# Keys and values of an encoder block: two plain products of x, or one product formed from seven quarter products

## The chip, the core and the metric

The kernel runs on one core of one Trainium2 chip. The metric is the device time in microseconds of one execution, taken as the median of several runs. The core has five engines with queues of their own: PE multiplies matrices (into PSUM), DVE (VectorE), ACT (ScalarE) and POOL (GpSimd) work on vectors of 128 partitions, and SP issues most of the transfers. An engine takes its instructions in the order of its queue, and one that waits holds up all behind it.

## What is computed

One layer of a bidirectional encoder on 1024 rows of 1024 columns, all in float32. What matters here is the combined projection of the normalised rows, and what its columns are for:

```python
h = rms(x, norm1_g)
p = h @ w_in                        # columns: qk of mLSTM, v, o, 16 gates, attention q, k, v
mix_a = mlstm_group(silu(dwconv(p_qk)), p_v, p_o, p_gates, ...)
mix_b = diff_attention_group(p_q, p_k, p_va, ...)    # q and k are normalised per head of 64
x = x + concat(mix_a, mix_b) @ w_out
x = x + square(relu(rms(x, norm2_g) @ w_ff1)) @ w_ff2
```

Of these columns, "values" below are the 512 of `p_v` (mLSTM), "keys" the 512 of the attention's k, "queries" the 512 of its q, and "gates" the 16 input and forget gates.

## The kernel before, in words

Every float32 product is made of three products of a shorter type: each operand is split into a high part (a copy by ACT that rounds to `F32R`) and a low part (operand minus high part, a subtraction by DVE or POOL), and PE adds high x high, high x low and low x high in PSUM. The factor `1/rms` of a row is not put on x but applied to the outputs (`rcol`, by rows; `rb`, the same copied to all partitions, by columns); the weight of the norm is put on x in the split.

The start of the kernel, which the change rewrites, goes in four parts.

Values. Eight PSUM banks `pv` hold the eight blocks of 128 rows. For each of the eight blocks k of 128 columns of x, SP loads `xT[k]`, ACT makes `hhi[k]` (line 221) and DVE `hlo[k]` (222), weights are loaded by pairs of k and split (171, 173, 174; the first pair by halves, with DVE's cast at 212), and PE adds 24 matmuls of 512 columns (239). Then the rows of x are loaded again in row order by POOL's queue (251), ACT sums their squares (252), DVE and POOL turn the sums to `rcol` (253, 89), POOL's queue stores them to DRAM and loads them again copied to all partitions, as `rb` (259, 260). The values are scaled by `rcol` as they leave PSUM and are stored to `vm_dram` (265 to 268).

Keys with gates. `key_weights` (404 to 406) loads and splits four tiles of 2 x 528 columns. For each block of rows PE makes two accumulations of 256 and 272 columns (`mm3`, lines 138 to 140); DVE takes the gates out (436), `head_norm` (339 to 349) copies the keys to SBUF, sums squares per head and scales. `head_turn` (368 to 381) transposes the normalised keys and stores them.

Queries. `row_block` does the same with four tiles of 2 x 512 columns. Between their matmuls, `step()` lets the pending generators go on, one piece at a time: the turns of keys, then `gates()`, which transposes the gates, scans them and stores the rows that the mLSTM heads load later.

After this, `proj` and `columns` form the convolution's inputs, one tile of 128 columns at a time. In that part the order on the engines is written out by hand: `when(t, f)` puts a piece of work at a time of the code's clock, which goes on by one every 12 matmuls, and the pieces are issued in the order of these times.

In the first three parts the order of the work is that of the program text, as far as the framework's own ordering keeps it. The tiles take their room from pools by tags; a tile that takes the room of another waits until all reads and writes of that one are done.

## Time and profile before

| what | value |
|---|---|
| median of 3 runs | 1238.62 us (1238.03 to 1239.58) |
| the profiled execution's own time | 1239.08 us |
| its span, first to last instruction | 1236.9 us |
| granted TensorE clock, mean over the span | 1.000 |
| ACT busy | 621.7 us (50%) |
| SP's queue (q1) | 154.11 MB, 38.8% of the transfer engines' time |
| POOL's queue (q0) | 25.70 MB |
| DMA in all | 212.77 MB, 172 GB/s |

A row of the timeline reads: start in us, duration in us, engine, line of the code, operation, output tile <- input tiles, shapes, how many instructions the row merges, and in brackets how long the engine had been idle and for whom. A row of the groups reads: line, engine, operation, tiles and shapes, count, then busy time in us and the mean of one in ns, then the idle time before them and who ended it. A row of the waits reads: engine, tile and line, the one waited for, then us in total, how often, and the longest. The durations of PE's matmuls overlap (a row of 0.39 us follows the last by 0.23), so a matmul's cost is taken from start to start.

### The profile page before, as it was taken

The numbers are of one execution on the slowest core, as the hardware profiler recorded it, in microseconds if no ns is written. First come the engines' busy times: TensorE is split into PE (matmuls) and PEld (weight loads), VectorE is DVE, ScalarE is ACT, GpSimd is POOL, SyncE is SP. The second block draws the span as 40 slices with busy tenths as digits, with TensorE's granted clock in tenths as the row PEclk, the third lists the DMA queues.
The fourth block names the chain that finished last, engine by engine and source line by source line (L and its number), as shares of the span: only waits on it lengthen the run. The fifth ranks groups of instructions, "written<-read, shape, count | busy, mean of one in ns | idle before, by whom it ended". The sixth has DMA issues, their size and how long they took to land.

```text
span 1236.9 us, 17075 instructions
## 1 busy us (share of the span) xinstructions
PE 1228.3 (99%) x6397; PEld 1029.4 (83%) x6397; DVE 817.0 (66%) x1154; ACT 621.7 (50%) x1070; POOL 240.7 (19%) x268
## 2 busy tenths in 40 slices
PE   9999999999999999999999999999999999999998
PEld 8998788888878878888887888888888888888887
DVE  6335668895267796774789886766655765468654
ACT  7334437777356676664465454454544433333332
POOL 1133513473334363321000000000000000014001
PEclk9999999999999999999999999999999999999999
DMA  9514262364364585526545773534459655445732
GB/s 346 207 41 165 45 226 81 113 157 123 124 223 160 167 287 162 177 92 234 184 145 166 244 247 136 170 130 157 148 212 343 245 165 193 147 132 163 221 111 94
DMA packets 102750, 212.77 MB, mean 172 GB/s; under 512 B 9096, under 2 KB 21896, under 8 KB 102664
## 3 DMA queue, kind: packets, MB, share of 16 engines
q1 hardware_dynamic: 78164, 154.11, 38.8%
q10 hardware_dynamic: 15272, 31.89, 6.7%
q0 software_dynamic: 9232, 25.70, 6.3%
q8 instruction: 50, 0.82, 0.3%
q14 instruction: 32, 0.26, 0.1%
HBM read 153.36 MB, written 58.30 MB: 171 GB/s over the span
## 4 chain that ended last, share of the span: by engine, by line
PE 90%; DVE 4%; DMA 2%; ACT 1%; issue 1%; POOL 1%; ACTq 0%; SPq 0%; DVEq 0%; POOLq 0%
PE z L1746 8%; PE z L1745 8%; PE z L1744 8%; PE m L1415 7%; PE m L1417 7%; PE m L1416 7%; PE pav L1018 4%; PE pva L889 4%; PE pv L239 4%; PE pl L978 4%; PE pw L138 3%; PE pw L140 2%; PE pw L139 2%; PE pj_c L138 2%; PE pj_c L140 2%; PE pj_c L139 2%
## 5 line engine op out<-in xcount | busy, mean ns | idle before, releaser
L1789 POOL TENSOR_TENSOR zx<-zx,res 128x512 f32<-128x512 f32 x4 | 8.7, 2181 | 492.0 <-DVE zx L1787 492.0
L1746 PE MATMUL z<-wbh,wa0l 128*128 128x512 f32 x224 | 87.4, 390 | 0.1
L983 DVE CUSTOM_DVE_ANT_0 l<-pl,toe 128x1024 f32<-128x1024 f32 x64 | 76.3, 1221 | 16.6 <-PE pl L978 15.9
L1744 PE MATMUL z<-wbh,wa0h 128*128 128x512 f32 x224 | 87.2, 389 | 0.0
L1745 PE MATMUL z<-wbl,wa0h 128*128 128x512 f32 x224 | 87.1, 389 | 0.0
L1745 PE MATMUL z<-wel,wa1h 128*128 128x512 f32 x224 | 87.1, 389 | 0.0
L1744 PE MATMUL z<-weh,wa1h 128*128 128x512 f32 x224 | 87.1, 389 | 0.0
L1746 PE MATMUL z<-weh,wa1l 128*128 128x512 f32 x224 | 87.1, 389 | 0.0
L1328 ACT ACTIVATE wbh<-g 128x1024 fp32r<-128x1024 f32 x28 | 29.7, 1061 | 90.2 <-PE z L1746 53.0
L1328 ACT ACTIVATE weh<-g 128x1024 fp32r<-128x1024 f32 x28 | 29.7, 1061 | 90.2 <-PE z L1746 53.4
L989 ACT ACTIVATE l<-l,sm 128x1024 f32<-128x1024 f32 x64 | 73.2, 1149 | 0.5 <-DVE sm L983 0.5
L1331 DVE TENSOR_TENSOR wel<-g,weh 128x1024 fp32r<-128x1024 f32 x28 | 35.2, 1257 | 56.6 <-ACT weh L1328 56.6
L1464 ACT ACTIVATE sq<-sq 128x512 f32<-128x512 f32 x48 | 30.2, 630 | 82.5 <-DVE sq L1503 65.7
L1331 DVE TENSOR_TENSOR wbl<-g,wbh 128x1024 fp32r<-128x1024 f32 x28 | 35.4, 1265 | 53.5 <-ACT wbh L1328 53.3
L1018 PEld LDWEIGHTS pav<-v,at 128*128 128x128 f32 x512 | 61.5, 191 | 3.4 <-issue 1.1
L1018 PE MATMUL pav<-v,at 128*128 128x128 f32 x512 | 62.7, 275 | 0.0
L978 PE MATMUL pl<-kk,q 64*128 64x512 f32 x384 | 55.3, 410 | 0.9 <-DVE sm L983 0.9
L138 PE MATMUL pj_c<-hhi,w_c 128*128 128x512 f32 x128 | 53.1, 414 | 0.0
L138 PE MATMUL pw<-mix,hi_wo 128*128 128x512 f32 x128 | 52.0, 406 | 0.0
L140 PE MATMUL pj_c<-hhi,w_c 128*128 128x512 f32 x128 | 50.3, 393 | 0.0
L139 PE MATMUL pj_c<-hlo,w_c 128*128 128x512 f32 x128 | 50.1, 391 | 0.0
L140 PE MATMUL pw<-mix,lo_wo 128*128 128x512 f32 x128 | 50.0, 391 | 0.0
(450 smaller groups left out, 3575.1 us busy)
## 6 DMA issues: line engine op xcount, KB each, us to landing
g<-g_dram SPq DMA_DIRECT2D x56, 512.0 KB, 3.9
g_dram<-gs SPq DMA_DIRECT2D x64, 256.0 KB, 4.4
g_dram<-sq ACTq DMA_DIRECT2D x42, 256.0 KB, 2.2
kk<-k_dram POOLq DMA_DIRECT2D x16, 512.0 KB, 6.0
raw_wo<-in_w_o_dram SPq DMA_DIRECT2D x16, 512.0 KB, 4.9
re<-in_w_dram SPq DMA_DIRECT2D x16, 512.0 KB, 4.4
ro<-in_w_dram SPq DMA_DIRECT2D x16, 512.0 KB, 3.8
zt<-in_w_dram SPq DMA_DIRECT2D x16, 512.0 KB, 3.9
```

Source lines behind the costliest of these rows:

```text
L138: nc.tensor.matmul(out, ahi, bhi, start=start, stop=False)
L139: nc.tensor.matmul(out, ahi, blo, start=False, stop=False)
L140: latest[0] = nc.tensor.matmul(out, alo, bhi, start=False, stop=stop).ins
L978: nc.tensor.matmul(it.pl[x][:, sl], hd.q[r, i, qi * P : (qi + 1) * P], hd.kk[r, j, sl], start=n == 0, stop=n == 2)
L983: nc.vector.tensor_tensor_reduce(lt, it.pl[m], hd.toe[:, off : off + S], 1.0, 3.0e38, ALU.add, ALU.min, it.sm[:, m : m + 1])
L1018: nc.tensor.matmul(it.pav[:, 0:P], at, it.head.v[:, c], start=c == 0, stop=c == NC - 1)
L1415: nc.tensor.matmul(p, wh, xh, start=go, stop=False, skip_group_check=True)
L1416: nc.tensor.matmul(p, wh, xl, start=False, stop=False, skip_group_check=True)
L1417: nc.tensor.matmul(p, wl, xh, start=False, stop=stop and k == 3, skip_group_check=True)
L1744: nc.tensor.matmul(p, wh, gh, start=go, stop=False, skip_group_check=True)
L1745: nc.tensor.matmul(p, wh, gl, start=False, stop=False, skip_group_check=True)
L1746: nc.tensor.matmul(p, wl, gh, start=False, stop=end, skip_group_check=True)
```

## The change

Keys and values are computed together. With x cut into quarters (rows 0 to 511 and 512 to 1023; columns 0 to 511 and 512 to 1023: A11, A12, A21, A22) and the weights of keys and of values each cut into an upper and a lower half (k0, k1; v0, v1), the four output quarters are formed from seven products of quarters instead of eight. Eight of the fourteen operands are sums: of x, A21+A22, A11-(A21+A22), A11-A21 and A12+A11-(A21+A22), each times the norm's weight; of the weights, v0-k0, v0-k0-v1, v1-v0 and v0-k0-v1+k1 (`t1` to `t4`). Each sum is split into high and low part like any operand.

The seven products go into eight PSUM banks, four `X` and four `Z`. Keys of the upper rows are products one and two; the others come from running sums that ACT copies out of `X` and DVE adds to `Z`. Product six adds into the banks of `Z` that hold product three, after these have been read (`keep3` and the sum behind it). Each product is 16 groups of three matmuls of 512 columns.

The order of this part is written out by hand on all engines: `at(t, f)` collects pieces of work, and they are issued in the order of their times t, which are planned microseconds. `pe(p, i)` is the planned time of group i of product p (both from 0). A core of the diff; it is cut at the marks.

```diff
+    order.enter_context(tc.manual_schedule())
...
+        G = 0.682
+        T0 = 5.0
+
+        def pe(p, i):
+            return T0 + G * (16 * p + i)
...
+        def hi(dst, x, g=None):
+            if g is None:
+                nc.scalar.activation(dst[0], x, AF.Copy)
+            else:
+                nc.scalar.activation(dst[0], x, AF.Copy, scale=g)
+
+        def lo(dst, x, eng=nc.vector):
+            eng.tensor_tensor(dst[1], x, dst[0].bitcast(F32), op=sub)
+
+        def lo_g(dst, x, g):
+            nc.vector.scalar_tensor_tensor(dst[1], x, g, dst[0].bitcast(F32), op0=mult, op1=sub)
...
+        def vt(out, a, b, op, eng=nc.vector):
+            eng.tensor_tensor(out, a, b, op=op)
+
+        def mul_add(out, x, g, y, op=add):
+            nc.vector.scalar_tensor_tensor(out, x, g, y, op0=mult, op1=op)
...
+        for j in range(4):
+            t = 18.5 + 2.6 * j
+            at(t, hi, (hs[j],), x22[j], g1[4 + j])
+            at(t + 0.5, vt, kr[j], v0[j], kr[j], sub, nc.gpsimd)
+            at(t + 0.6, hi, A22[j], x22[j], g1[4 + j])
+            at(t + 0.8, mul_add, hs[j], x21[j], g1[j], hs[j])
+            at(t + 1.6, hi, SB[j], hs[j])
+            at(t + 1.7, lo_g, A22[j], x22[j], g1[4 + j])
+            at(t + 1.9, whi, "t1", j, kr[j])
+            at(t + 2.3, lo, SB[j], hs[j])
+            at(t + 2.6, wlo, "t1", j, kr[j], nc.gpsimd)
...
+        for j in range(4):
+            at(29.0 + 1.4 * j, mul_add, hs[j], x11[j], g1[j], hs[j], sub)
+            at(29.8 + 1.4 * j, hi, A21[j], hs[j])
+            at(30.5 + 1.4 * j, lo, A21[j], hs[j])
...
+        for j in range(4):
+            at(31.0 + 1.3 * j, lambda j=j: vt(kr[j], kr[j], v1[j], sub, nc.gpsimd))
+            at(32.6 + 1.5 * j, whi, "t2", j, kr[j])
+            at(33.5 + 1.5 * j, wlo, "t2", j, kr[j])
...
+        for j in range(4):
+            at(36.0 + 1.3 * j, vt, d[j], x11[j], x21[j], sub, nc.gpsimd)
+            at(41.0 + 1.3 * j, lambda j=j: vt(v0[j], v1[j], v0[j], sub, nc.gpsimd))
+            at(38.5 + 1.4 * j, hi, SB[j], d[j], g1[j])
+            at(39.2 + 1.4 * j, lo_g, SB[j], d[j], g1[j])
+            at(42.2 + 1.4 * j, whi, "t3", j, v0[j])
+            at(46.5 + 1.3 * j, wlo, "t3", j, v0[j], nc.gpsimd)
+            at(44.5 + 0.8 * j, mul_add, x12[j], x12[j], g1[4 + j], hs[j])
...
+            at(50.5 + 0.1 * j, load_k1, j)
+            at((40.5, 49.0)[j // 2] + 0.8 * (j % 2), lambda j=j: whi("v1", j, v1[j]))
+            at(51.7 + 1.3 * j, lambda j=j: wlo("v1", j, v1[j], nc.gpsimd))
+            at(50.5 + 1.0 * j, hi, A21[j], x12[j])
+            at(51.2 + 1.0 * j, lo, A21[j], x12[j])
+            at(57.0 + 1.3 * j, lambda j=j: vt(kr[j], kr[j], k1b[j], add, nc.gpsimd))
+            at(59.5 + 1.3 * j, whi, "t4", j, kr[j])
+            at(62.2 + 1.3 * j, wlo, "t4", j, kr[j], nc.gpsimd)
...
+        plan = (
+            (X, A11, "k0", True, False), (Z, A12, "k1", True, True), (Z, SB, "t1", True, False),
+            (X, A21, "t2", False, False), (X, SB, "t3", False, False), (Z, A21, "v1", False, True),
+            (X, A22, "t4", False, True),
+        )
...
+        for t in range(4):
+            e = lambda p, t=t: pe(p, 9.9 + 2 * t) + 0.3
+            at(e(0), lambda t=t: nc.scalar.activation(zs[0][:, t], X[t], AF.Copy))
+            at(e(1), lambda t=t: nc.vector.tensor_tensor(zs[0][:, t], Z[t], zs[0][:, t], op=add))
+            at(e(3), keep, t)
+            at(e(4), keep3, t)
+            at(e(4) + 0.7, lambda t=t: nc.vector.tensor_tensor(vr[4 + t], Z[t], vr[4 + t], op=add))
+            at(e(5), values, t)
...
+        for t in range(NC):
+            at(41.3 + 2.6 * t, row_load, t)
+            at(44.0 + 2.6 * t, row_square, t)
+        at(63.0, row_factor)
+        at(65.5, row_turn)
...
+        for i, (slot, t1, t2) in enumerate(((0, 67.3, 70.2), (1, 67.4, 71.6), (2, 72.9, 74.6), (4, 76.0, 77.4))):
+            at(t1, query_room, i, slot)
+            at(t2, lambda i=i: hi(wqg[i], wqg[i][2]))
+            at(t2 + 1.2, lambda i=i: lo(wqg[i], wqg[i][2]))
```

`row_turn` is the store of the row factors and the load of `rb`, still on POOL's queue; row slices of x are now loaded by SP's queue (`row_load`). Half of the keys' weights and a quarter of x are loaded a second time (`load_k1`, `load_x21`). The query weights' raw tiles take the room of `kr`, the raw weights of keys in which the sums of weights are formed.

Behind this part the loop that formed keys with gates forms queries with gates, in the same shapes and with the same `step()`; `row_block` is gone. The keys, which already lie in SBUF, are normalised by `key_norm`, the squares with the row factor as scale. The first piece of `gates()` runs ahead of `proj`, and its other pieces are put into the hand-written table of the part after it:

```diff
+    for n in range(9):
+        heapq.heappush(table, (0.3 + 1.2 * n, 10**6 + n, next, (gate_steps, None)))
```

More of the change, by code (lines that the diff above doesn't have):

```diff
@@ new lines, in key_norm, with end @@
+    def key_norm(t):
+        zt = zs[t // 4][:, t % 4]
+        sq = kgp.tile([P, 8, 64], F32, tag="zsq", name=f"zsqk{t}", bufs=2)
+        nc.scalar.activation(sq.rearrange("p a b -> p (a b)"), zt, AF.Square, scale=rcol[:, t : t + 1])
+        ss = kgp.tile([P, 8], F32, tag="zss", name=f"zssk{t}", bufs=2)
+        nc.vector.tensor_reduce(ss, sq, axis=mybir.AxisListType.X, op=ALU.add)
+        last = nc.vector.tensor_scalar(ss, ss, 64 * EPS, None, op0=ALU.add)
+        rsqrt(ss, ss, 8)
+        with tc.issue_after(last.ins):
+            norm_end()
+        z8 = zt.rearrange("p (a b) -> p a b", b=64)
+        def end():
+            nc.vector.tensor_scalar(ss, ss, rcol[:, t : t + 1], None, op0=ALU.mult)
+            nc.vector.tensor_tensor(z8, z8, ss[:, :, None].to_broadcast([P, 8, 64]), op=ALU.mult)
+        ends.append(end)
@@ L575, in hybrid_block_kernel @@
+        if t == 4:
+            pending.append(head_turn(kgp2, "zz", 4, zs[1], 1, False))
+            pending.append(head_turn(kgp2, "zz", 4, zs[2], 0, True))
+    norm_end()
+    gate_steps = gates()
+    next(gate_steps)
     pj0 = proj(w_c[4], "c4")
```

360 lines of the change are left out of this document (218 added, 142 removed).

## Prediction

> **What bounds the kernel now.** I read the page's busy shares first, then the waits of PE, then PE's timeline around the changed stage.
>
> ```profile
> span 1236.9 us, 17075 instructions
> PE 1228.3 (99%) x6397; PEld 1029.4 (83%) x6397; DVE 817.0 (66%) x1154; ACT 621.7 (50%) x1070; POOL 240.7 (19%) x268
> ```
>
> ```profile
> PE pv L199 <- POOL ones L76: 1.1, 1, 1.1
> ```
>
> PE is busy 99% of the span, and the longest wait that any PE instruction has is 1.1 us, at the very start. So the end is set by the number of matrix columns that PE streams: a matmul taken away anywhere is worth its whole pitch, and any microsecond in which PE is made to wait is lost in full. Both halves of that sentence decide this change.
>
> The chain of waits and PE's timeline give the stage's parts:
>
> ```profile
> 5.17 43.84 PE pv L239 x192
> ```
>
> ```profile
> 48.84 0.28 PE L138 MATMUL pkg<-w_kg,hhi 128*128 128x256 f32 x1
> ...
> 96.90 0.29 PE L140 MATMUL pkg<-w_kg,hlo 128*128 128x272 f32 x1
> 97.49 0.39 PE L140 MATMUL pqa<-w_qa,hlo 128*128 128x512 f32 x1
> 98.17 0.39 PE L140 MATMUL pqa<-w_qa,hlo 128*128 128x512 f32 x1
> ```
>
> The values are 192 matmuls of 512 columns from 5.17 to 48.84: 43.67/192 = 0.2274 us each, 0.68 per group of three (97.49 to 98.17 is the same step among the queries). Keys with gates run from 48.84 to 97.2 in 384 matmuls of 256 and 272 columns, with 16 transposes between. The queries after them are again 192 matmuls of 512.
>
> How full the helpers are is in the windows of the stage (columns: window, length, then busy time of PE, PEld, DVE, ACT, POOL, granted clock, DMA share, GB/s):
>
> ```profile
> 0.00:10.00 10.00, 8.71 (x39) 7.70 (x40) 4.63 (x8) 5.70 (x8) 1.11 (x11) 1.00 0.79 276
> 10.00:20.00 10.00, 10.00 (x46) 8.29 (x45) 8.88 (x15) 7.71 (x9) 1.29 (x2) 1.00 1.03 411
> ...
> 60.00:70.00 10.00, 10.00 (x85) 10.00 (x85) 3.41 (x8) 2.64 (x4) 2.86 (x2) 1.00 0.01 2
> ```
>
> While values run, DVE is busy 8.88 of 10 us; while keys run, only 3.41. The present stage has its vector work early and little later on; POOL does 1.3 to 2.9 us in ten.
>
> **PE's work.** Keys and values are each 8 x 8 x 512 columns times three: 384 matmuls, 384 x 0.2274 = 87.3 us. Seven quarter products of 16 (block, row) pairs times three are 336, or 76.4 us. Gates with queries have the shapes and the count that gates with keys had, so they cancel, and so do the transposes of keys and queries. PE's saving is 48 x 0.2274 = 10.9 us. With PE alone, keys and values that start at 5.17 end at 92.5 before and at 81.6 after.
>
> **The first product.** It starts later.
>
> ```profile
> 3.44 0.43 DVE L212 CAST w_v<-raw_v 128x512 fp32r<-128x512 f32 x1 [2.61 <-DMA raw_v<-in_w_v_dram]
> 4.39 0.72 ACT L221 ACTIVATE hhi<-xt,vecs 128x512 fp32r<-128x512 f32 x1 [1.72 <-DMA xt<-in_xT_dram]
> 6.62 0.63 ACT L230 ACTIVATE w_v<-raw_v 128x512 fp32r<-128x512 f32 x1
> 8.01 1.43 DVE L222 SCALAR_TENSOR_TENSOR hlo<-xt,vecs,hhi 128x512 fp32r<-128x512 f32 x2
> ```
>
> Now DVE casts the first weights (3.44) while ACT is still waiting for x, and the first matmul goes 5.17, when ACT's 0.72 is over. After the change ACT casts both, x and then weights (0.63 more), and the second matmul wants the weights' low part, which DVE makes after x's (0.75, then 0.69). 0.63 for the first and about half a microsecond for the second: I take 1.1 us.
>
> **The sums, and the port they share.** This term decides. Behind the first two products stand operations that before doesn't have: sums of quarters and the splits of these sums. I counted them in the diff, in the order of their times, since the order on every engine is fixed. POOL has 36 operations of 128x512 with two SBUF inputs (20 plain sums; 16 low parts). DVE has 36 of them, from the first sum of x to the last low part before the values' first sum: 16 plain ones, 20 with a scalar. Alone they cost:
>
> ```profile
> L222 DVE SCALAR_TENSOR_TENSOR hlo<-xt,vecs,hhi 128x512 fp32r<-128x512 f32 x4 | 2.9, 751 | 1.4 <-ACT hhi L221 1.4
> L231 DVE TENSOR_TENSOR w_v<-raw_v,w_v 128x512 fp32r<-128x512 f32 x2 | 1.4, 687 | 0.0
> ```
>
> ```profile
> L1144 POOL TENSOR_TENSOR mm<-so,mm 128x512 fp32r<-128x512 f32 x8 | 10.4, 1297 | 27.6 <-ACT mm L1143 27.6
> ```
>
> By these rows both engines would keep up: 36 x 1.297 = 46.7 us on POOL in the 50 us that the order gives it. But look at what DVE and POOL do when both run such operations:
>
> ```profile
> 1125.05 8.01 POOL L1792 TENSOR_TENSOR res<-res,zv 128x512 f32<-128x512 f32 x4
> ```
>
> ```profile
> 1104.66 1.22 DVE L1331 TENSOR_TENSOR wa1l<-zt,wa1h 128x1024 fp32r<-128x1024 f32 x1
> 1105.79 0.68 DVE L1787 TENSOR_TENSOR zx<-zv,z 128x512 f32<-128x512 f32 x1
> ...
> 1111.24 0.68 DVE L1787 TENSOR_TENSOR zx<-zv,z 128x512 f32<-128x512 f32 x1
> 1111.83 1.22 DVE L1704 TENSOR_TENSOR zt<-za,zd 128x1024 f32<-128x1024 f32 x1
> ...
> 1125.28 2.14 DVE L1331 TENSOR_TENSOR wel<-g,weh 128x1024 fp32r<-128x1024 f32 x1 [1.35 <-ACT weh L1328]
> 1127.35 2.31 DVE L1331 TENSOR_TENSOR wa1l<-zt,wa1h 128x1024 fp32r<-128x1024 f32 x1
> 1129.58 2.32 DVE L1704 TENSOR_TENSOR zt<-za,zd 128x1024 f32<-128x1024 f32 x1
> 1131.82 2.32 DVE L1331 TENSOR_TENSOR wbl<-g,wbh 128x1024 fp32r<-128x1024 f32 x1
> 1134.06 1.21 DVE L1331 TENSOR_TENSOR wa0l<-zt,wa0h 128x1024 fp32r<-128x1024 f32 x1
> ```
>
> DVE's steps of 128x1024 take 1.13 us from start to start when POOL is idle (1104.66 to 1105.79). While POOL makes four sums, the same steps come 2.24 apart (1127.35, 1129.58, 1131.82, 1134.06), and as soon as POOL is done they cost 1.21 again. 1125.28 to 1134.06 is 8.78 us; less four DVE steps of 1.13 leaves 1.07 for each POOL sum. They don't overlap at all: they alternate. The same holds for 512 columns:
>
> ```profile
> 212.41 0.69 DVE L805 TENSOR_TENSOR to<-to,nd 128x512 f32<-128x512 f32 x1
> 213.02 2.07 DVE L670 SCALAR_TENSOR_TENSOR k<-pad,vecs,k 128x1024 f32<-128x1024 f32 x1
> ```
>
> ```profile
> 212.51 1.50 POOL L804 TENSOR_TENSOR to<-to,nd 128x512 f32<-128x512 f32 x1 [5.38 <-DVE nd L802]
> ```
>
> POOL asks at 212.51, gets in when DVE's 0.69 is over, and DVE's next stands until POOL is done (2.07). An operation that reads PSUM has no part in this:
>
> ```profile
> 217.21 1.23 DVE L666 TENSOR_TENSOR pad<-pj_c,rb 128x1024 f32<-128x1024 f32 x1 [0.26 <-PE pj_c L140]
> ```
>
> ```profile
> 218.00 1.05 POOL L804 TENSOR_TENSOR to<-to,nd 128x512 f32<-128x512 f32 x1
> ```
>
> So the cost of the sums is the *sum* over both engines. A DVE step of 512 is 0.59 plain (1111.24 to 1111.83) and 0.68 with a scalar (8.01, two in 1.43, less the tail); a POOL sum is 1.07, and a POOL low part I put at 1.2 (1.297 alone, less a tenth for what overlaps).
>
> What waits for them? Product six adds into the banks that hold product three, so it can't start before the lower value rows have been read out there. That read is a DVE sum, and DVE's order puts all 36 operations ahead of it. POOL's, alternating, have then done 32: 20 sums and 12 low parts (its first 24 feed products three to five; the next eight only take their turns). Start: POOL's first sum needs the first quarter of the value weights, which stands behind 5.1 MB on the load queue. The windows moved 2.76 MB in the first 10 us and 411 GB/s after, so 15.8 us, and I take 17. Then 16 x 0.59 + 20 x 0.68 = 23.0, and 20 x 1.07 + 12 x 1.2 = 35.8: the queue is through at 75.8, and with the sum itself product six starts at 76.5. PE by itself would start it at 5.17 + 1.1 + 240 x 0.2274 = 60.9. PE therefore idles some 15.6 us, part of it at product four, whose weights' low part is DVE's twentieth operation here. Products six and seven take 21.8 more: 98.3 us, against 92.5 before. The stage has lost 5.8 us instead of winning 10.9.
>
> [...] By whole durations the 68 operations would be about 62.6 us instead of 58.8, and the sum 3.8 us worse; the trace's own steps (2.24, not 2.31) speak for the smaller figure.
>
> **Query weights.** All four are loaded into two raw buffers that the last sum of weights occupies, and that sum's last low part on POOL now stands behind the stores of the row factors and the load of their copies:
>
> ```profile
> 42.55 2.07 POOL L259 DMA_DIRECT2D r_dram<-rrow  x4 [0.74 <-DVE rrow L257]
> 48.06 0.56 POOL L260 DMA_DIRECT2D rb<-r_dram  x1 [3.44 <-DMA r_dram<-rrow]
> ```
>
> ```profile
> raw_qa<-in_w_qa_dram SPq DMA_DIRECT2D x4, 512.0 KB, 3.7
> ```
>
> ```profile
> L405 ACT ACTIVATE w_kg<-raw_kg 128x1056 fp32r<-128x1056 f32 x4 | 4.2, 1076 | 3.3 <-DMA raw_kg<-in_w_kg_dram 3.3
> L252 ACT ACTIVATE xr<-xr 128x1024 f32<-128x1024 f32 x8 | 8.4, 1054 | 3.2 <-DMA xr<-in_xR_dram 3.2
> L252 ACT ACTIVATION_READ_ACCUMULATOR xr<-xr 128x1 f32 x8 | 1.5, 184 | 0.0
> ```
>
> ```profile
> L406 DVE TENSOR_TENSOR w_kg<-raw_kg,w_kg 128x1056 fp32r<-128x1056 f32 x4 | 4.9, 1247 | 5.0 <-ACT w_kg L405 5.0
> ```
>
> That is 2.07 + 3.44 + 0.56 = 6.1 us on POOL, then two rounds of load 3.7, high part 1.08, low part 1.25: 12 us. With POOL's last low part at about 92, the fourth pair is ready near 104; queries that start at 98.3 want it after six of their 64 steps of 0.72 (the keys' 48 us, less their transposes), at 102.6. So 0 to 3 us; I take 1. Gates now follow in small pieces under the convolution's projections; they have the same few matmuls as before, and the rows they store (at 6.3 of the code's clock) are loaded at 14.5: nothing, or at most a microsecond at their first two transposes, if PE stands behind DVE there. Row squares and PSUM copies on ACT change place, not number, but see the third rival.
>
> **Sum.** -10.9 + 1.1 + 15.6 + 1.0 = +6.8 us. The profiled execution took 1239.08 (span 1236.9), the median of the runs is 1238.62; from the median, 1245.4. I say 1245.5. About 0.2%, 2.5 us, is what a measurement of this kernel can tell from none.
>
> **The rivals.**
> First, DVE wins the ties. If a queue of ready DVE operations went ahead of POOL each time, only the 24 POOL operations that feed products three to five need come first: 16 x 1.07 + 8 x 1.2 = 26.7 instead of 35.8, product six at 67.4, and with the query weights the change is -2.3: 1236.4, no change. The alternation at 1125 to 1134 speaks against it.
> Second, PE's clock. The granted clock is 1.00 in each window above, but PE never waits over 1.1 us there, and after the change it would for 5 to 8 us twice. If the clock fell to a half for as long again as the waits, the 12 us would cost 6 more: 1251.5. [...] No row of before can show it.
> Third, the other side: the port doesn't decide, since the two engines seldom meet (POOL's order may sit in the gaps where DVE waits for ACT). Then ACT's queue is late: four squares of row slices, 1.05 and their read 0.18, lie among the PSUM copies of product five that product six waits for. -10.9 + 1.1 + 4 x 1.23 = -4.9: 1233.7, faster. It decides once more than about 6 of DVE's 23 us get through beside POOL: then the 58.8 shrink to 52.7, product six starts at 70.4 and the stage ends at 92.2, even with before. For it: either engine alone would fit. Against: 58.8 us of such work in the 43 before product six is due leave few gaps.
> Fourth, all of the saving arrives: -9.8, or 1228.8. It needs that nothing above is late.
>
> **How the numbers follow.** The forecast 0.48, the clock on top 0.13, DVE first 0.14, ACT only 0.15, all saved 0.10. Slower: 0.61; the same: 0.14; faster: 0.25. The range leaves out the fourth rival and a little above the second: 1230 to 1252. The slower case's own range is 1241 to 1252: POOL's unit between 1.0 and 1.2 moves the sum by 3 us either way.
>
> **What would show it.** Right: PE's waits name a DVE sum at the values' banks ahead of product six, 5 to 8 us, and a DVE low part of weights ahead of product four; between 20 and 75 us, two-input DVE steps of 512 average 1.5 us or more and POOL's over 1.5; the query loop begins near 98 us, or a few later. Wrong: DVE's means stay at 0.69 and 0.75 there, PE's longest wait is under 2 us, and queries begin by 83 to 88. A granted clock under 1.00 between 45 and 85 us would be the second rival.

## The result, and the profile after

The changed kernel takes 1271.18 us (median of 4 runs, 1270.4 to 1275.23), beside 1239.09 for the kernel before on the same chip: ratio 1.0267, 95% interval 1.0244 to 1.029. That is 32 us slower. The prediction had the direction (slower) and the place of the largest term, but 1245.5 with a range up to 1252, so four fifths of the loss were not in it.

The profiled execution took 1275.23, the longest of the four, 4 us over their median; its span is 1273.4, 36.5 more than before. The page of the changed kernel, its span and busy time:

```profile
span 1273.4 us, 17177 instructions
PE 1236.1 (97%) x6349; PEld 1031.2 (81%) x6349; DVE 864.8 (68%) x1206; ACT 647.1 (51%) x1127; POOL 290.2 (23%) x296
```

PE has 48 instructions fewer, as the count of columns said, and is busy 8 us longer: matmuls at a granted clock of 0.50. Where the 36.5 us lie is read from the first matmul of each part (rows by tile), in us from the span's start, for some of the kernels below:

| kernel | first `pj_c` | from there to first `pva` (convolutions, mLSTM) | first `pl` to first `m` (attention) | span |
|---|---|---|---|---|
| before | 144.4 | 124.2 | 271.2 | 1236.9 |
| after | 164.4 | 135.6 | 277.2 | 1273.4 |
| sums on DVE (1) | 147.4 | 135.0 | 277.6 | 1257.1 |
| before, gates late (2) | 143.5 | 130.4 | 271.3 | 1242.0 |
| even slot count (5) | 161.2 | 133.2 | 271.5 | 1262.3 |
| four repairs (14) | 146.8 | 132.2 | 271.4 | 1247.2 |

The start up to `pj_c` lost 20.0 us, the convolutions 11.4, the attention 6.0; the rest gave back 0.9. Of the 20.0, the products have 16.7 (queries begin at 109.2; at the pitch of before, 384 matmuls from 5.17 on would have been through at 92.5) and the queries 3.3.

PE's waits in the changed kernel, first up to 125 us, then from 125 to 310 us (engine, tile and line, the one waited for; us in total, times, longest):

```profile
PE pv L392 <- DVE w_t L266: 5.0, 1, 5.0
PE pvz L392 <- DVE vr L443: 3.4, 2, 2.7
PE pv L392 <- ACT u L414: 3.2, 2, 2.1
PE pv L392 <- ACT w_t L261: 2.0, 1, 2.0
...
PE pqa L138 <- ACT w_qa L261: 1.5, 1, 1.5
...
PE pqa L139 <- DVE bt L615: 0.9, 1, 0.9
PE pqa L139 <- DVE w_qa L266: 0.8, 2, 0.6
PE pvz L392 <- DVE z L440: 0.7, 2, 0.5
```

```profile
PE pj_c L140 <- POOL w_c L834: 2.5, 1, 2.5
PE pzTrue L591 <- DVE zzTrue L599: 1.8, 1, 1.8
PE pe L689 <- DVE er L692: 1.7, 1, 1.7
```

Before, no wait of PE was over 1.1 us. Now there are ten or so, and PE pays twice for many of them. The windows of the changed kernel, cut on a raster of 3.41 us (columns: window, length, busy time of PE, PEld, DVE, ACT, POOL, then granted clock, DMA share, GB/s), show how:

```profile
43.81:47.22 3.41, 1.23 (x5) 0.45 (x3) 3.41 (x3) 1.15 (x2) 3.41 (x3) 1.00 0.00 0
47.22:50.64 3.42, 0.00 (x0) 0.00 (x0) 3.42 (x3) 1.95 (x4) 3.42 (x3) 0.50 0.00 0
50.64:54.05 3.41, 1.99 (x5) 1.61 (x6) 3.41 (x3) 3.13 (x6) 3.41 (x3) 0.50 0.51 156
54.05:57.46 3.41, 3.41 (x10) 2.63 (x9) 3.41 (x3) 2.15 (x4) 3.41 (x3) 0.50 0.56 154
57.46:60.88 3.42, 3.42 (x17) 2.80 (x16) 3.42 (x3) 0.77 (x2) 3.42 (x3) 1.00 0.44 127
...
81.36:84.77 3.41, 0.72 (x3) 0.30 (x3) 0.69 (x1) 2.70 (x6) 0.97 (x1) 1.00 0.22 55
84.77:88.18 3.41, 3.31 (x8) 2.13 (x8) 1.29 (x2) 2.75 (x6) 1.28 (x1) 0.50 0.82 258
...
187.17:190.58 3.41, 1.68 (x12) 0.98 (x11) 2.98 (x10) 0.03 (x1) 0.00 (x0) 1.00 0.62 249
190.58:193.99 3.41, 3.41 (x10) 2.63 (x9) 2.15 (x5) 2.23 (x3) 0.00 (x0) 0.50 0.33 133
```

The stretches in which PE worked 1.23, 0.72 and 1.68 of 3.41 us are each followed by one at a clock of 0.50; in the one at 54.05, where PE was busy throughout, lie 10 matmuls, against 17 in the one at 57.46. The third pair is a wait of only 1.7 us (1.73, ahead of `pe`). Up to 310 us there are eight such half-speed stretches, against none before; half of PE's busy time in them is lost. From the rows above that is (0 + 1.99 + 3.41 + 3.31)/2 for four of the five in the products; with 3.41/2 for the fifth, at 71.1, it makes 6.1 us.

The timeline of PE shows half pace at the start too, where the profile's clock reads 1.00:

```profile
1.12 4.21 PE L215 MATMUL pv<-ones 128*128 128x128 f32 x18 [1.12 <-POOL ones L76]
6.90 1.66 PE L392 MATMUL pv<-w_k,hhi 128*128 128x512 f32 x2 [1.56 <-ACT w_k L261]
...
10.06 1.05 PE L392 MATMUL pv<-w_k,hhi 128*128 128x512 f32 x2
10.92 0.63 PE L392 MATMUL pv<-w_k,hlo 128*128 128x512 f32 x1
...
13.54 0.63 PE L392 MATMUL pv<-w_k,hhi 128*128 128x512 f32 x2
14.01 0.39 PE L392 MATMUL pv<-w_k,hlo 128*128 128x512 f32 x1
```

Two matmuls take 0.86 us at 10.06 and 0.47 at 13.54. PE begins at half pace in every trace here: from 2 to 3 us and from 3 to 4 us each of the 17 has 7 and 6 of the warm-up's small matmuls in work. Before, too, they come 0.21 us apart, and 0.11 apart from 4.5 us on. In the changed kernel they come 0.21 apart to their end at 5.3, the first product starts at 6.90 and runs at 0.43 a matmul to 13.1: 2.6 us lost. Part of this belongs to this one execution. In the kernels of 1, 4, 5 and 6, whose start is the same, the first product came at 5.9 to 6.0, since x landed 1.0 us earlier, and half pace ended between 6.0 and 10.4. Experiment 1:

```profile
5.89 0.53 PE L392 MATMUL pv<-w_k,hhi 128*128 128x512 f32 x1 [0.56 <-ACT w_k L261]
...
7.33 0.62 PE L392 MATMUL pv<-w_k,hhi 128*128 128x512 f32 x2
7.79 0.39 PE L392 MATMUL pv<-w_k,hlo 128*128 128x512 f32 x1
```

There the pace was full from the second matmul on.

### The profile page after: what moved, and what is told of

Same layout as the page of the kernel before. It is cut to its first block, busy times and chain, and to the rows that moved or that the text cites. A ratio compares the mean times of both kernels' runs of the same rounds, so it can differ in the third digit from the quotient of the medians.

```text
span 1273.4 us, 17177 instructions
## 1 busy us (share of the span) xinstructions
PE 1236.1 (97%) x6349; PEld 1031.2 (81%) x6349; DVE 864.8 (68%) x1206; ACT 647.1 (51%) x1127; POOL 290.2 (23%) x296
```

## The experiments

Ratios are to the kernel before, measured beside each, with 95% intervals. The kernel before had medians of 1239.1 to 1239.9 in all of them.

**1. All sums on VectorE.** The theory on trial: POOL's sums cost DVE their whole time, since the two alternate. Nine calls in the text, 36 operations, change the engine:

```diff
-            at(t + 0.5, vt, kr[j], v0[j], kr[j], sub, nc.gpsimd)
+            at(t + 0.5, vt, kr[j], v0[j], kr[j], sub, nc.vector)
```

> The changed kernel with all 36 sums and low parts of POOL moved to DVE, in the same order. Theory (the two engines alternate on a port, and PE's clock falls in the waits this makes): the same operations cost 0.59 instead of 1.07 to 1.2 us each, product six starts at 62 to 66 us instead of 84.5, queries begin at 84 to 90 instead of 109, no window under a clock of 0.95 after 20 us, and the whole comes to 1247 to 1253. Rival (too much vector work for the stage, on whatever engine): DVE takes the place of POOL, product six starts after 78 us, and the whole stays at 1265 or more.

Measured: 1257.43 (1256.42 to 1258.9), ratio 1.0143 (1.0128 to 1.0158). So 13.7 us come back by taking work away from an idle engine and giving it to the fuller one. The groups from 17 to 85 us, in the changed kernel, DVE and POOL (busy us, mean ns of one):

```profile
L266 DVE TENSOR_TENSOR hlo<-hs,hhi 128x512 fp32r<-128x512 f32 x4 | 7.1, 1764 | 0.0
L281 DVE SCALAR_TENSOR_TENSOR hs<-xta,vecs,hs 128x512 f32<-128x512 f32 x4 | 7.0, 1772 | 0.0
L440 DVE TENSOR_TENSOR z<-pvz,z 128x512 f32<-128x512 f32 x4 | 2.7, 678 | 0.0
```

```profile
L278 POOL TENSOR_TENSOR raw_k<-raw_k,xtw 128x512 f32<-128x512 f32 x4 | 6.8, 1732 | 0.0
L278 POOL TENSOR_TENSOR xtxb<-xta,xtxb 128x512 f32<-128x512 f32 x4 | 6.7, 1714 | 0.0
```

And in this experiment, the same two groups of DVE:

```profile
L281 DVE SCALAR_TENSOR_TENSOR hs<-xta,vecs,hs 128x512 f32<-128x512 f32 x4 | 2.9, 747 | 0.0
L266 DVE TENSOR_TENSOR hlo<-hs,hhi 128x512 fp32r<-128x512 f32 x4 | 2.8, 689 | 0.0
```

Beside each other the two need 1.75 us for one step each; DVE alone needs two steps of 0.6 to 0.75 for the same. The sum that reads PSUM (L440) stays at 0.68. The alternation is shown; what makes the two alternate, which the prediction calls a port, no trace shows. The queries began at 95.6, not at 84 to 90 as expected, half speed (0.50) still came, at 57.2 and 70.8, and the total lies between theory and rival: more was late than the alternation made late. Of the 13.6 us by which the queries come earlier than in the changed kernel's profile, 3.5 lie ahead of 13.2 us, in a start that is the same in both; the sums are worth about 10 in these two executions.

**2. Gates late, in the kernel before.** Only the gates' pieces are moved as the change moves them:

```diff
-    pending.append(gates())
...
+    gate_steps = gates()
+    next(gate_steps)
...
+    for n in range(9):
+        heapq.heappush(table, (0.3 + 1.2 * n, 10**6 + n, next, (gate_steps, None)))
```

> The kernel before with one part of the change alone: the gates' pieces behind the first run in the hand-written table, under the convolution's projections. Theory (the order of the pieces itself makes PE wait for DVE there, about 4 us of waits and as much again by a lower clock): 1244 to 1249, with PE waits at the gates' small matmuls. Rival (the loss between 164 and 300 us in the changed kernel is handed on from its late first stage): within 2 us of before.

Measured: 1242.62 (1241.63 to 1244.82), ratio 1.0025 (1.0014 to 1.0036). In the profiled execution the convolutions take 130.4 us instead of 124.2, and 0.9 is won ahead of them. PE's waits from 125 to 300 us:

```profile
PE pj_c L140 <- POOL w_c L624: 2.2, 1, 2.2
PE pe L491 <- DVE er L494: 1.8, 1, 1.8
```

These are waits that the changed kernel has too, and a half-speed stretch follows the first. So late gates have a price of their own, without any quarter product: 6 us of this part in this execution, 3.2 us in the medians, which is less than the theory had and more than the rival.

**3 and 4. More warm-up matmuls; the gates' small matmuls ahead of their copies.** Both on top of 1:

```diff
-        for _ in range(9):
+        for _ in range(13):
```

```diff
-        for i, (src, dst) in enumerate(((u, ucol), (ws, wcol), (fl, fcol))):
-            nc.tensor.transpose(pt[:, i * 64 : i * 64 + 64], src, ident[0:64, 0:64])
-            nc.vector.tensor_copy(dst, pt[:, i * 64 : i * 64 + 64])
+        for i, src in enumerate((u, ws, fl)):
+            nc.tensor.transpose(pt[:, i * 64 : i * 64 + 64], src, ident[0:64, 0:64])
+        for i, dst in enumerate((ucol, wcol, fcol)):
+            nc.vector.tensor_copy(dst, pt[:, i * 64 : i * 64 + 64])
```

> As the run with all sums on DVE, with 13 instead of 9 matmuls of ones ahead of the first product, so that PE is busy until about 6.7 us and hardly waits before its first real matmul at 6.9. Theory (a wait of 1.6 us already lowers the clock: the first 13 matmuls came at 0.43 us): these come at 0.23, 2.5 to 3 us are won in the first product, and if nothing later takes it back, in the whole. Rival (the first product waits for loads and splits): the pace of the first groups and the whole stay within 0.5 us of the run without it.

> As the run with all sums on DVE, and in gates() the two and three small matmuls that share a bank go ahead of the copies of their results, so that PE doesn't wait for a copy between them. Theory: the waits of 1.7 and twice 0.4 us there go, and with the first the slow matmuls behind it (1.7 us): 3 to 5 us under the run without it, 1243 to 1249. Rival (DVE is simply late there and another wait takes their place): under 1 us.

Measured: 1255.22 (1253.81 to 1259.01), ratio 1.0129 (1.0111 to 1.0147), and 1256.27 (1255.53 to 1259.02), ratio 1.0137 (1.0122 to 1.0152). Against 1 that is 2.2 and 1.2 us, within the spread of the runs. The first product of 3 began at 5.99 at full pace, but so did that of 1, at 5.89: the loss that 3 was to take away wasn't in the execution that it is compared with, and the queries came 0.5 us earlier. What more warm-up is worth is therefore not shown. The traces only say that half pace ended between 6.0 and 13.1 us in the five kernels with the changed kernel's warm-up, and by 7.3 in the nine with 13. In 4 the waits of `pe` and `pt` are gone, as expected, and little came of it.

**5. Even slot count.** The attention part lost 6 us in after, 1, 3 and 4, and nothing in 2, though its code and the order of its instructions are the same. In the changed kernel ACT's timeline shows where:

```profile
398.23 1.06 ACT L128 ACTIVATE w_o<-raw_o 128x1024 fp32r<-128x1024 f32 x1 [8.52 <-PE po L140]
```

ACT waits 8.5 us with the weights of the third output gate, because the tile's room is still read by PE for another gate. The same conversion before:

```profile
358.19 1.06 ACT L128 ACTIVATE w_o<-raw_o 128x1024 fp32r<-128x1024 f32 x1
```

`w_tiles` counts its calls and takes the count modulo five, later, when two slots are left, modulo two. Before, 12 tiles had been taken by the time of `proj`; the changed kernel sets the count there by hand, to 3. The next tile goes where it should, but 12 tiles later the count is odd instead of even, and the third gate takes the slot of the second instead of the first.

```diff
-    wturn[0] = 3
+    wturn[0] = 8
```

> The changed kernel with one number different: the count that picks weight slots after the first stage starts at 8 instead of 3 (the same slot of five, but an even count once only two slots are left). Theory: the 6 us that the attention part lost come from the third output gate's weights landing on the slot that the second gate's product still reads; then ACT's wait of 8.5 us ahead of that conversion and PE's 3.9 us at the attention products are gone, the attention part takes about 306 us instead of 312, and the total is 1263 to 1267. Rival, that the layout of the new tiles or the later gates cost it: the part stays at 312 and the total within 1270 to 1273.

Measured: 1266.68 (1264.26 to 1267.61), ratio 1.0213 (1.0198 to 1.0228); the attention takes 271.5 us and the waits of ACT and PE there are gone. From 366 to 640 us PE's waits in the changed kernel, and in this one:

```profile
PE pav L1231 <- ACT at L1223: 3.9, 1, 3.9
PE pl L1191 <- DVE sm L1196: 0.9, 2, 0.6
```

```profile
PE pl L1191 <- DVE sm L1196: 0.9, 2, 0.6
```

The only other wait there is one of 0.2 us. The cause is shown: one number, 4.5 us in the medians, 6 in the profile.

**6. Zero products in PE's longest wait.** Does the clock have a price of its own in the stage? A matrix of zeros is multiplied ahead of product four, on the changed kernel, so that PE is busy while it waits:

```diff
+                if p == 3 and i == 0:
+                    at(pe(p, i) - 0.001, lambda: [
+                        nc.tensor.matmul(X[0][:, 0:P], zero, ones, start=False, stop=False, skip_group_check=True)
+                        for _ in range(30)
+                    ])
```

> The changed kernel with 30 small matmuls of a zero matrix (which add nothing to their bank) ahead of product four, where PE sat idle for 7 us out of 44.5 to 52. Nothing else waits less. Theory A, the clock has a price of its own: PE runs at full speed from 52 to 57 instead of half, and the queries begin 2.5 to 4 us earlier; total 1267 to 1269. Theory B, VectorE's late steps set every later wait: the clock is full there, but PE waits as much longer ahead of products five and six, the queries begin within 0.7 us of before, total 1270 to 1272.

Measured: 1273.28 (1270.17 to 1276.06), ratio 1.0268 (1.0246 to 1.0289): no gain. The clock stayed at 1.00 there until 64 us, but PE then waited elsewhere (up to 125 us):

```profile
PE pv L394 <- ACT u L421: 4.3, 2, 3.9
PE pvz L394 <- DVE vr L450: 2.8, 2, 2.1
...
PE pv L394 <- DVE w_t L268: 1.0, 2, 0.6
```

The 5.0 us are down to 1.0, the next wait is up from 3.2 to 4.3, and new half-speed stretches follow it. The queries began at 106.5, 2.7 earlier than in the changed kernel's profile, which by itself would speak for theory A; but they began at 106.2 in 5, the same stage with nothing filled, and the total has no gain. So for this wait theory B stands: between products four and six PE's speed is not what sets the end, DVE and ACT are. Where no helper is late behind it (behind the stage's last waits, in the queries, in the convolutions) I count half speed as lost, up to 1.7 us a stretch, half of 3.41; that is an estimate, which no run measures by itself.

**7 and 8. Another order; gates first.** On 1, 3, 4 and 5 together, 7 puts later what product five doesn't need, and 8 also runs the gates beside `proj`:

```diff
-            at(44.5 + 0.8 * j, mul_add, x12[j], x12[j], g1[4 + j], hs[j])
+            at(50.41 + 1.0 * j, mul_add, x12[j], x12[j], g1[4 + j], hs[j])
...
-        at(46.0, parameters)
+        at(58.0, parameters)
...
-            at(44.0 + 2.6 * t, row_square, t)
+            at(44.0 + 2.6 * t if t < 4 else 60.0 + 0.7 * (t - 4), row_square, t)
```

```diff
-    gate_steps = gates()
-    next(gate_steps)
+    pending.insert(0, gates())
```

> All sums and low parts of the stage on VectorE, 13 warm-up matmuls, the gates' small matmuls ahead of their copies, the even slot count, and three things later in the stage's hand-written order: the four sums that only product six needs, the parameters, and the last four row squares (behind the copies that product six waits for). Theory: the waits ahead of products five (3.1 us) and six (about 3.5 us) came from that order, and with them go the half-speed stretches behind them: total 1240 to 1246, queries near 88. Rival, VectorE is simply full from 20 to 64 and the wait only moves on: what is left is the slot's 6 us, total 1247 to 1251.

> The kernel of e7, with the gates' pieces run first in the list that is worked off beside the projection of the first keys, instead of out of the hand-written table. Theory: in the table they hold up ACT, VectorE and GpSimd, which run in order, at a price of 6 us; without them the convolution part takes 124 to 126 us, and the projection and what is drained behind it 2 to 4 us more: total 2 to 4 us under e7. Rival: the turns of queries that the gates push back have nothing beside them, and the stretch up to the convolutions grows by 6 or more: total equal to e7 or up to 5 us above.

Measured: 1254.84 (1254.44 to 1255.65), ratio 1.0121 (1.0106 to 1.0136), and 1261.11 (1260.01 to 1263.54), ratio 1.0174 (1.0159 to 1.0189). Both are misses, 5.6 and 11.8 us above the kernel that they build on (14, below). In 7 the wait for DVE's low parts ahead of product five is gone, but the row factor comes later (ACT scales the first values at 81.5, in 3 at 78.9), DVE stands 4.5 us for POOL's step of the keys' norm, the query weights' low part is queued behind that, and PE waits 3.2 us for it at 94 us. In 8 the gates' chain stands in the open: PE waits 4.7 us for a step of it, then runs at half speed to 178 us.

**9 to 12.** All four build on 14. 9 was to form the low parts of later weights on POOL ahead of its masks, 10 forms the gates from a constant beside the queries (the columns that belong to them are left unused, so its output isn't the layer's), 11 has the edits of 9, the two first of 7, and four loads of rows on POOL's queue, 12 is 11 with the last four sums of weights on POOL.

```diff
-            load(xr[t].rearrange("p a b -> p (a b)"), xR[t])
+            load(xr[t].rearrange("p a b -> p (a b)"), xR[t], nc.gpsimd if t >= 4 else nc.sync)
```

> All sums on VectorE, 13 warm-up matmuls, the gates' small matmuls ahead of their copies, the even slot count (together, from the runs so far, 1249 to 1251), and one thing more: GpSimd forms the low part of each later projection's weights right behind ACT's high part, ahead of its masks, instead of behind them. Theory: late gates make the masks wait for the gates' rows, and the low part waits behind the masks, so PE waits 1.6 to 3.4 us for it and then runs 3.4 us at half speed; with this the wait is gone, the convolution part takes about 127 us, total 1245 to 1248. Rival, that the masks are then late themselves and hold up the product of queries and keys: no gain, 1249 to 1252.

> The same base without that (1249 to 1251), and the gates formed from a constant, beside the queries, in the list that is worked off there as in the kernel before; the columns that the matmuls give are copied but not used, so the output is not the reference's. It gives the price of forming the gates behind the queries. Theory: the convolution part goes back to 124 to 125 us from 130, and the stretch of the queries stays within 1 us: total 1243 to 1246. Rival, that the convolution part's loss is from the weights' slots or the layout: it stays at 129 to 131, total 1249 to 1251.

> The kernel with the low parts early, and in the stage: the four sums for product six and the parameters later, and the last four loads of rows issued by GpSimd's queue instead of behind the loads of weights and quarters that wait for their buffers. Theory: ACT's square no longer waits 5.2 us for its rows ahead of the copies of product five's banks, product six starts 2 to 4 us earlier, the query weights are not late as they were when the squares came behind those copies: queries near 91, total 1239 to 1244. Rival, VectorE full: queries at 94 to 96, total as without it, 1245 to 1248.

> The kernel of that order, with the four sums of weights for product seven on GpSimd again, where VectorE is idle (64 to 70). Theory: off VectorE's queue they no longer hold up the sums of values that product six waits for, and there are only four of them beside VectorE: 0.5 to 2 us faster than without. Rival: they alternate with VectorE's low parts at 1.75 us a pair, and it is 1 to 3 us slower.

Measured: 1252.17 (ratio 1.0098, 1.0083 to 1.0113), 1255.99 (1.0134, 1.0117 to 1.0151), 1252.09 (1.0097, 1.0081 to 1.0113), 1253.43 (1.0117, 1.0102 to 1.0133). None is a gain on 14. 9 did not do what it was meant to: the masks also stand ahead of the high part in that order, and PE still waits 3.7 us there. 10 moved the gates' waits into the queries (59.6 us up to `pj_c`, against 51.7 in 14) and a wait of 3.4 us for a turn of keys to the start of the convolutions, which stayed at 131.4, against 132.2 in 14. That is near the number of the rival, which had the loss there from other causes than the gates; what stands there now is another wait, so 10 doesn't decide between the two. 11 took away the waits ahead of product five, and product six waited 4.2 us instead. In 12, POOL's timeline and DVE's show another form of what POOL's sums cost DVE:

```profile
70.56 2.48 POOL L278 TENSOR_TENSOR raw_k<-raw_k,xtk 128x512 f32<-128x512 f32 x2
```

```profile
69.76 3.33 DVE L96 TENSOR_SCALAR cst<-vecs 128x4 f32<-128x4 f32 x1
73.00 0.16 DVE L97 TENSOR_SCALAR cst<-vecs 128x4 f32<-128x4 f32 x1
```

A step of four elements, 0.16 us by itself, stood 3.33 us until both sums were through (it began beside an earlier sum of POOL, and didn't end in the 0.5 us between that one and these), with the values' sum behind it; product six waited 8.1 us.

**13. Waits of many lengths, in the kernel before.** This was to measure by itself which waits half speed follows.

```diff
+        nc.tensor.matmul(p[0:64, 0:64], ones[0:1, 0:64], ones[0:1, 0:64], start=True, stop=True)
+        nc.vector.tensor_copy(line[:, 0:64], p[0:1, 0:64])
+        for _ in range(n):
+            nc.vector.tensor_scalar(line, line, 1.0, None, op0=ALU.mult)
+        nc.tensor.matmul(p[0:64, 64:128], ones[0:1, 0:64], line[:, 0:64], start=True, stop=True)
```

> The kernel before, with some thirty waits of different lengths put into its loops of keys and of queries, where PE otherwise runs without a pause at full clock: a small matmul, a chain of 1 to 20 small steps on VectorE that starts from it, and a small matmul that waits for the chain. The outputs stay those of the reference. Theory: the clock is set anew every 3.41 us, at half if PE was busy for less than about half of the stretch that has just ended; so waits under 1.6 us are never followed by half speed, waits of 3.4 us and more always, those between now and then, by where they lie, and the changes of the clock all fall on one raster of 3.41 us. Rival: only a wait that fills a whole stretch of 3.4 us brings half speed, and no wait under 3.4 us does. Second rival: any wait over 1.6 us does.

Measured in one execution: 1274.21 us. Most of the waits didn't come about, because the framework's order put other matmuls between the two small ones. Two long ones are left in the loops, of 3.29 us at 112.2 and of 1.81:

```profile
169.01 0.32 PE L287 MATMUL gap<-line,ones 1*64 1x64 f32 x2 [1.81 <-DVE line L286]
```

The others are 1.2 or less. Half speed followed both long ones, from 114.6 to 121.5 and from 169.2 to 176.1, and none of the short. That speaks against the first rival, by which no wait under 3.4 us does it. It doesn't part the theory from the second rival, any wait over 1.6 us; for that the changed kernel has a wait of 1.8 us ahead of `pzTrue`, at 174.3, with no half speed behind it.

**14 and 15. The four repairs alone; the gates' pieces wider apart** (1.8 instead of 1.2):

```diff
-        heapq.heappush(table, (0.3 + 1.2 * n, 10**6 + n, next, (gate_steps, None)))
+        heapq.heappush(table, (0.3 + 1.8 * n, 10**6 + n, next, (gate_steps, None)))
```

> The changed kernel with all sums on VectorE, 13 warm-up matmuls, the gates' small matmuls ahead of their copies and the even slot count, and nothing more: what the last four kernels were built on. If the four parts add (13.7, 1.1 to 2.2, 1.2 and 4.5 us off 1271.2), 1249 to 1251; that is what those kernels were compared with. Rival: they overlap, 1252 to 1254, and then the low parts formed earlier and the other order were worth 1 to 2 us after all.

> The same, with the pieces of the gates 1.8 steps of the hand-written order apart instead of 1.2. Theory: a piece whose inputs are not ready holds up VectorE and ACT in order; wider apart, PE's waits for the turn of queries (1.8 us) shrink by 1 us or more, while the gates' rows land later, and GpSimd's masks and the low part behind them with them: within 2 us of the base, the loss only changing place. Rival: the spacing is the whole trouble, 3 to 5 us faster.

Measured: 1249.28 (1247.4 to 1250.13), ratio 1.008 (1.0065 to 1.0095), and 1252.74 (1252.12 to 1252.78), ratio 1.011 (1.0093 to 1.0127). The repairs add: 13.7 + 2.2 + 1.2 + 4.5 = 21.6 expected, 21.9 measured; since two of the four are no larger than the spread of the runs, that it fits so well is partly luck. Wider spacing is 3.5 us worse than the base, beyond what was given as the theory's bound: now PE waits 5.2 us for a state step of DVE. 14 is the fastest version of the changed kernel, and still 10 us slower than the kernel before. Its four largest sums of waits, up to 300 us:

```profile
PE pv L392 <- DVE w_t L266: 3.1, 1, 3.1
PE pvz L392 <- DVE vr L443: 2.4, 4, 1.0
PE pzTrue L591 <- DVE zzTrue L599: 2.1, 2, 1.8
PE pj_c L140 <- POOL w_c L836: 2.0, 1, 2.0
```

## Why the prediction was wrong

The alternation came out near its forecast. What failed is that the sum went no further than the waits: it put half speed behind them and the late gates at nothing, and didn't follow the weight slots past the query weights.

**PE's saving, -10.9: right.** 48 instructions fewer, and at full clock a group of three still takes 0.68 us.

**First product, +1.1: about right, but for this execution.** In 1, 4, 5 and 6 it came 0.7 to 0.8 us later than before, and its second and third matmul stood some 0.6 us more for low parts. In the changed kernel's profile it came at 6.90 instead of 5.17, 1.7 later, with the same 0.6 behind it. Half pace to 13.1 us, another 2.6, isn't in the forecast's term at all: before, it had ended with the warm-up.

**The sums on two engines, +15.6: right in that they alternate, near in size partly by luck.** Product four waited for a DVE low part (5.0), product six for DVE's sum at the values' banks, though 2.7 and not 5 to 8, and PSUM sums stayed at 0.68. Groups that ran wholly beside each other had means of 1.76 on DVE and 1.73 on POOL; over all two-input steps of 512 between 20 and 75 us the means are 1.31 and 1.64, so DVE's misses the mark of 1.5 that was given. PE's waits in the products, without the first, add to 14.3 (the first four rows of the waits above and 0.7). A pair of steps took 1.75 us; by the prediction's own prices it is 1.66 (0.59 and 1.07), by whole durations 1.99 (0.69 and 1.30). (For the 68 operations whole durations add to 67.5 us by the rows that the prediction shows, not to its 62.6.) What failed is the last link. The timelines of DVE and of ACT in the changed kernel:

```profile
73.41 6.55 DVE L266 TENSOR_TENSOR hlo<-xtxc,hhi 128x512 fp32r<-128x512 f32 x4 [3.94 <-ACT hhi L261]
83.74 0.69 DVE L443 TENSOR_TENSOR vr<-pvz,vr 128x512 f32<-128x512 f32 x1 [3.79 <-ACT vr L420]
```

```profile
82.07 1.06 ACT L456 ACTIVATE xr<-xr 128x1024 f32<-128x1024 f32 x1 [6.09 <-DMA xr<-in_xR_dram]
...
83.13 0.58 ACT L420 ACTIVATE vr<-pv 128x512 f32<-128x512 f32 x1
```

DVE's queue was through at 80.0 instead of 75.8, after a wait of 3.9 for ACT; then the sum for product six stood 3.8 us for ACT's copy, which is queued behind the square of a row slice that waited 6.1 us for its rows. So product six began at 84.5, not 76.5, and its last wait was for rows of x, not for DVE's queue. The load of these rows stood on SP's queue behind one that waited for ACT until 69.8, so the lateness of the sums may be in it too; no run parts the two. The third rival's lateness of ACT came on top of the alternation, not in its place. And DVE alone, in 1, doesn't bring the stage back: after 20 us it is full, and the stage still ends later than before.

**The clock: the step that failed first.** The sum had half speed at nothing and kept it as a rival with a chance of 0.13 and a price of 6 us for two long waits. In the trace it follows a wait of 1.7 us too. That it lasts as long again as the wait, from which that price is worked out, no run shows: behind the 5.0 us ahead of product four the clock read 0.50 from 47.2 to 57.5, with PE at work in the last 5.4 us of it, and behind the 2.7 ahead of product six from 84.8 to 88.2. Of the 16.7 us by which the products are late, -10.9 + 1.7 + 14.3 leaves 11.6, from start to start of the matmuls: half pace is 2.6 at the start and 6.2 in the later stretches, 0.6 are the low parts of the first product, 1.4 comes of counting the eight waits from the end of the matmul before, 0.16 or so behind its pitch (0.39 against 0.23), and 0.8 is spread. Further on there is one such stretch in the queries, two in the convolutions and one in the attention, worth up to 1.7 us each. Up to 310 us the clock fell six times, each time behind a stretch of 3.41 us in which PE was still busy for a fifth to a half (0.72 to 1.73 us); in the attention it fell behind one with 0.12. Experiment 6 bounds the term from the other side: at the wait that it filled, where DVE is late anyway, half speed cost nothing that it could tell.

**Gates, "nothing, or at most a microsecond": wrong by 5 at least, by 10 if all of the part's loss is theirs.** The convolutions lost 11.4 us: waits of 2.5, 1.8, 1.7 and three of 0.4, less the 0.9 that this part had before, are 6.3, and two half-speed stretches 3.4; 1.7 are spread. The prediction priced when the gates' rows are needed and left out that their pieces stand in the queues of engines that run in order. Experiment 2 shows it with 6.2 us in this part, and there ends what is shown: in the kernels that have the new start and the gates in this part it lost between 6.3 (4) and 12.1 us (6), and no run parts the other 5 us of 11.4 from that start. Beside the queries of the new start they cost about as much (10); 13, where they stand as before, has this part at 124.7.

**Query weights, +1: too small.** The queries lost 3.3: PE waits of 1.5 and 0.8 for the last weights, 0.9 behind the small steps of the distance bias on DVE, and a half-speed stretch of up to 1.7. That is 4.9; the gates' pieces, which left this part, give back some (0.9 in 2), and 0.7 stays open.

**The attention: not in the prediction.** 6.0 us by a slot count set by hand (5). The change sets the number, and the prediction followed the slots no further than the query weights.

In sum: -10.9 for the saving, 1.7 for the start, 14.3 waits and the 11.6 of the products (8.8 of them half pace), 3.3 queries, 11.4 convolutions, 6.0 attention, 0.9 given back: 36.5. These are the sizes of one execution, the longest of four; in the medians the loss is 32. What stays open are the small rests that no row names (0.8, 0.7 and 1.7 us) and how much of the convolutions' 11.4 belongs to the gates beyond 6.2.

## What to carry to other kernels

Where PE runs without a pause, a saving of matmuls that puts work on the helpers is priced with every new wait of PE counted as the wait and, at the worst, up to 1.7 us more for each stretch of 3.41 at half speed behind it. In the changed kernel such stretches followed single waits of 1.7 to 3.9 us, the 2.0 and 5.0 ahead of product four, and pairs of 2.1 with 1.1 and of 1.5 with 0.9, but not one wait of 1.8; where DVE was late right behind, half speed cost nothing that 6 could tell. Sums on POOL are no free work while DVE has two-input work from SBUF: count both engines as one (here 1.75 us for a pair of steps, where DVE alone took 0.6 to 0.75 for each), and don't expect a gain even where DVE's queue looks empty: in 12 the four sums put there were 1.3 us slower, within the spread of the runs. When a change moves or renumbers allocations, follow each rotating slot to the end of the kernel: the cost may appear 300 us later, in code that nobody touched.

## What the runs showed of the hardware that was not expected

**The clock's raster.** In each of the 16 traces with half speed, all changes of the granted clock up to 320 us fall on one raster of 3.413 us, to 0.01 us; its first mark behind the span's start lies at another time in each run, from 0.01 to 2.91 us. Counted on these rasters, over all 16, from the first full pace to 320 us: a stretch at full clock in which PE was busy for 0.44 or less was followed by half speed 33 times out of 33; for 0.56 to 0.93, 0 out of 142; between, 10 out of 25, and there the busy share doesn't tell which (in the changed kernel 0.47 at 173.5 us stayed at full speed, 0.49 at 187.2 didn't). Full speed came back behind 43 of 46 half-speed stretches that were busy for 0.88 or more, and behind none of 19 that were busy for 0.81 or less. So in the changed kernel the wait of 1.73 us ahead of `pe` was followed by half speed, worth up to 1.7 us, and the one of 1.79 ahead of `pzTrue` by none. The products of the changed kernel and of 5, which are the same code, ended at 109.2 and 106.2, of which 1.0 is the later load of x and most of the rest half pace. This is a count over traces, not an experiment of its own; 13 was meant as one and gave only two waits that bear on it. What sets the clock, the traces don't show.

**Sums on POOL and small steps.** A step of 4 elements on DVE, 0.16 us by itself, stood 3.33 us beside two sums of POOL (12): in that one case the two did not alternate, and why isn't shown.
